# Token-major copy of the residual: 32x32 transposes on VectorE and block DMAs in place of TensorE transposes and ScalarE copies

## Chip, cores and metric

One core of a Trainium2 chip runs the whole program. The metric is the device time of one execution in microseconds (us). Engines: PE is TensorE's matmul, PEld its weight load, DVE is VectorE, ACT is ScalarE, POOL is GpSimd, SP is SyncE, whose queue issues most DMAs.

## What is computed

One decoder block on 512 tokens of width 1024, all in float32: a gated merge of a convolution branch and differential attention, added to the residual, then a SwiGLU feed-forward part, added again, and a last RMSNorm. The change touches the residual between the two additions:

```
x = x + merged @ w_out[l]                                  # the residual x1

h2 = rmsnorm(x, g_ffn[l])
ff = jax.nn.silu(h2 @ w_ffn_gate[l]) * (h2 @ w_ffn_up[l])  # D_FF = 2816
x = x + ff @ w_ffn_down[l]                                 # x1 is added here
return rmsnorm(x, g_final)
```

## The kernel before

Up to the down product the kernel keeps activations feature-major: a tile has 128 features on the partitions and the 512 tokens along the free dimension, and eight such tiles hold the width of 1024. The down product comes out token-major (128 tokens on the partitions, 512 features along the free dimension), so the residual `x1`, eight feature-major tiles, is needed once more as eight token-major tiles `x1t[(n, t)]` (`n` the half of the features, `t` the block of 128 tokens). `turn_x1` (line 947) makes them while the gate and up products run; lines 1025 and 1030 read them in the down product.

**Precision.** Each float32 product is made of three matmuls on fp32r operands: every operand is split into `hi` (a rounded copy, by ACT) and `lo` (the rest, a subtraction by DVE or POOL), and hi by hi, hi by lo and lo by hi are summed in PSUM. The text calls these three matmuls a triple.

**Weights.** `w_d` is a row of 146 units of 512 KB. `emit_dma` (line 314) loads one into a `wr` buffer (3 of them) through the SP queue; `emit_split` makes `wh` by ACT and `wl` by a subtraction, on DVE from unit 64 on and so in the whole feed-forward part (4 buffers each). `next_unit` (line 342) hands out unit i, and before that issues loads up to unit i+4 and splits up to unit i+2.

**Feed-forward part.** `chunkA` (line 405) runs one pair of 128 columns, the gate's and the up's, over the 1024 features: two weight units with 24 matmuls each, into two PSUM banks, which are of tag `mm` and of tag `at` by turns (`two`, line 904). The loop over `f` of 22 such pairs (the first stands ahead of it, line 989) is at lines 992 and 993. `evac_ff` takes each result out of PSUM on DVE, applies silu on ACT, multiplies on POOL, and splits the product (ACT copy, DVE subtraction) for the down product.

**Order.** The program is written as one order per engine by a planner: `model` keeps a clock for each engine from assumed costs (0.215 us for a matmul of 512 columns), and side work is a generator (`spawn`) that yields the planner's time at which it wants to go on. `run` calls `service` before every triple, and `service` lets a generator go on whose time has come by PE's clock, or by the time for which the next triple is ready if that is later. A DMA that is issued with `nc.sync.dma_start` directly, not through `load`, does not enter the planner's clocks. Each engine, and the SP queue, carries its instructions out in the order in which they were emitted.

Of the kernel before, what the change touches and what calls it, by code (L numbers as in the profile page):

```python
# [4 lines left out]
T = 512  # L5
D = 1024
P = 128
# [161 lines left out]
def build(nw):  # L169
# [6 lines left out]
    F32, F32R = mybir.dt.float32, mybir.dt.float32r  # L176
# [3 lines left out]
    nc = bacc.Bacc("TRN2", target_bir_lowering=False, num_devices=1, dynamic_dma_scratch_size=1024)  # L180
# [11 lines left out]
    V, S, G, PE = (Engine(model, e, n) for e, n in ((nc.vector, "dve"), (nc.scalar, "act"), (nc.gpsimd, "pool"), (nc.tensor, "pe")))  # L192
    need = model.need
    clk = model.clk

    with tile.TileContext(nc) as tc, contextlib.ExitStack() as homes:  # L196
# [3 lines left out]
        with tc.tile_pool(name="cn", bufs=1) as cn, \  # L200
# [5 lines left out]
            def nm(s):  # L206
                uid[0] += 1
                return f"{s}_{uid[0]}"
# [3 lines left out]
            def tl(tag, dt=F32, w=512):  # L212
                t = home[tag].tile([P, 542 if tag == "T2" else w], dt, name=nm(tag), tag=tag, bufs=BUFS[tag])
                model.alloc(tag, BUFS[tag], t)
                live[tag] = live.get(tag, 0) + 1
                return t
# [11 lines left out]
            def psum(tag):  # L228
                t = pp.tile([P, 512], F32, name=nm(tag), tag=tag, bufs=PBUFS[tag])
                model.alloc(tag, PBUFS[tag], t)  # L230
                return t
# [12 lines left out]
            tasks, now = [], [0.0]  # L244
# [54 lines left out]
            ident = cn.tile([P, P], F32, name="ident")  # L299
# [611 lines left out]
            x1, h2 = [], []  # L911
# [33 lines left out]
            x1t = {}  # L945

            def turn_x1():
                for n in range(2):
                    for t in range(4):
                        tp = psum("cv")  # L950
                        yield now[0] + 3.0
                        for c in range(4):
                            PE.transpose(tp[:, c * P:(c + 1) * P], x1[4 * n + c][:, t * P:(t + 1) * P], ident)
                        d = tl("T4")
                        S.copy(d, tp)
                        x1t[(n, t)] = d

            gf = [tl("T4") for _ in range(2)]
            for n in range(2):
# [29 lines left out]
            run(chunkA(h2, two(0), hold, True))  # L989
            drain_tasks()  # L990
            spawn(turn_x1())
            for f in range(1, NF):
                run(chunkA(h2, two(f), evac_ff(f)))
# [85 lines left out]
```

## Time and profile before

| | |
|---|---|
| runs | median 895.67 us, 894.81 to 900.02 |
| profiled execution | 895.89 us, span 894.1 us |
| mean granted clock of TensorE | 0.996 |
| PE, DVE, ACT, POOL busy, share of the span | 98%, 64%, 41%, 33% |
| gate and up products from `f` = 1 on (start of the transposes' stage) | 533.1 us to about 765 us |
| DMA, mean over the span | 95 GB/s |

The span runs from the first instruction of the program to the last; the rest of the execution lies around it. An engine's busy share is a mean over stages with different limits, so the stage of the change is read by itself, in windows of some 30 us. The chain is the work that ended last, followed back from the end; an instruction that isn't in it has time to spare. In the rows, PE's matmuls overlap: what one costs is read from the distance between starts or from the chain, not from its own duration. All lines of the program's compute appear as L142, since one helper records them; the tiles' names tell them apart (`T` stands for every activation tile, `at`, `mm`, `cv` for PSUM).

### The profile page before, as it was taken

What the parts mean: (1) busy time and instruction counts of PE and PEld (TensorE: products, weight loads), DVE (VectorE), ACT (ScalarE), POOL (GpSimd) and SP (SyncE); (2) the same over time, 40 slices, a digit from 0 to 9 for tenths busy, and PEclk for the clock granted to TensorE, in tenths of its full rate; (3) what the DMA queues carried; (4) which work ended last, traced back from release to release, by engine and by line L of the source; (5) the groups of instructions that cost most, each with busy time, mean ns of one, the idle gap of its engine ahead of it and who ended that gap; (6) DMA issues with size and microseconds to landing.
All of it is one profiled execution on the core that took longest, in us unless ns stands there. A gap on an engine that the chain in (4) does not pass through costs nothing.

```text
span 894.1 us, 11318 instructions
## 1 busy us (share of the span) xinstructions
PE 877.9 (98%) x4246; PEld 732.0 (82%) x4246; DVE 570.4 (64%) x961; ACT 368.9 (41%) x619; POOL 296.5 (33%) x370
## 2 busy tenths in 40 slices
PE   9999999999999999999999999999999999999996
PEld 7778989888888887688888888888888888888885
DVE  6699889889999899966765643433344444323323
ACT  7332236666666775433633433322233332221312
POOL 3785576667766357564000010111111111000001
PEclk9999999999999999999999999999999999999998
DMA  8223222222212222132224432222222222422302
GB/s 281 90 103 118 91 75 72 73 71 71 71 48 95 71 71 95 48 118 74 88 98 141 142 118 94 95 95 95 95 95 95 95 95 94 141 95 71 118 24 95
DMA packets 26584, 85.21 MB, mean 95 GB/s; under 512 B 3088, under 2 KB 4368, under 8 KB 26528
## 3 DMA queue, kind: packets, MB, share of 16 engines
q1 hardware_dynamic: 25376, 82.52, 27.0%
q10 hardware_dynamic: 1152, 1.97, 0.6%
q8 instruction: 33, 0.54, 0.2%
q14 instruction: 23, 0.19, 0.1%
HBM read 82.38 MB, written 2.10 MB: 94 GB/s over the span
## 4 chain that ended last, share of the span: by engine, by line
PE 86%; DVE 8%; ACT 3%; issue 1%; DMA 1%; SPq 0%; POOL 0%; POOLq 0%; ACTq 0%; DVEq 0%
PE mm L142 54%; PE at L142 28%; DVE T L142 5%; PE cv L142 4%; ACT T L142 2%; DVE cv L142 2%; DVE kz L142 1%; DMA wr<-wall 1%; DMA T<-xT 1%; ACT wh L142 0%; SPq L234 0%; POOL T L142 0%; ACT L142 0%; DVE sm L142 0%; POOLq L196 0%
## 5 line engine op out<-in xcount | busy, mean ns | idle before, releaser
L142 PE MATMUL mm<-T,wh 128*128 128x512 f32 x1360 | 425.9, 394 | 1.3 <-DVE T L142 1.3
L142 PEld LDWEIGHTS mm<-T,wh 128*128 128x128 f32 x1360 | 251.5, 189 | 55.7 <-issue 3.4
L142 PE MATMUL mm<-T,wl 128*128 128x512 f32 x680 | 266.1, 391 | 0.0
L142 POOL TENSOR_TENSOR wl<-wr,wh 128x256 fp32r<-128x256 f32 x244 | 189.5, 812 | 127.4 <-ACT wh L142 121.1
L142 ACT CAST wh<-wr 128x1024 fp32r<-128x1024 f32 (+1 forms) x151 | 149.7, 1016 | 82.1 <-PE mm L142 36.5
L142 POOL TENSOR_TENSOR T<-T,T 128x256 f32<-128x256 f32 (+1 forms) x97 | 91.4, 952 | 239.1 <-DVE T L142 221.9
L142 DVE SCALAR_TENSOR_TENSOR cv<-T,vec_sb,cv 128x512 f32<-128x512 f32 x232 | 160.6, 747 | 0.1
L142 PE MATMUL at<-T,wh 128*128 128x512 f32 x496 | 153.3, 390 | 0.0
L142 PEld LDWEIGHTS mm<-T,wl 128*128 128x128 f32 x680 | 128.0, 188 | 28.1 <-DVE wl L142 0.2
L142 DVE TENSOR_TENSOR wl<-wr,wh 128x1024 fp32r<-128x1024 f32 (+1 forms) x91 | 102.5, 1152 | 70.8 <-ACT wh L142 70.4
L142 DVE TENSOR_TENSOR T<-T,T 128x512 fp32r<-128x512 f32 (+2 forms) x115 | 88.9, 774 | 57.8 <-ACT T L142 56.2
L142 ACT CAST T<-T 128x512 fp32r<-128x512 f32 (+2 forms) x112 | 67.5, 618 | 122.0 <-POOL T L142 77.4
L142 PEld LDWEIGHTS at<-T,wh 128*128 128x128 f32 x496 | 92.7, 188 | 18.9
L142 DVE TENSOR_TENSOR T<-mm,T 128x512 f32<-128x512 f32 (+2 forms) x77 | 52.4, 683 | 81.1 <-PE mm L142 74.1
L142 PE MATMUL mm<-wh,T 128*128 128x256 f32 (+1 forms) x432 | 100.9, 316 | 0.0
L142 ACT ACTIVATE T<-T 128x512 f32<-128x512 f32 (+1 forms) x73 | 44.3, 622 | 130.9 <-DVE T L142 130.8
L142 PE MATMUL at<-T,wl 128*128 128x512 f32 x248 | 96.8, 390 | 0.0
L142 ACT ACTIVATE T<-T,sm 128x128 f32<-128x128 f32 (+3 forms) x100 | 55.9, 561 | 69.0 <-DVE sm L142 64.0
L142 PEld LDWEIGHTS mm<-wh,T 128*128 128x128 f32 x432 | 73.2, 190 | 5.5
L142 DVE TENSOR_TENSOR T<-at,T 128x512 f32<-128x512 f32 (+4 forms) x59 | 38.2, 650 | 59.7 <-PE at L142 54.9
L142 PE MATMUL mm<-wl,T 128*128 128x256 f32 (+1 forms) x216 | 68.2, 316 | 0.0
L142 PEld LDWEIGHTS at<-T,wl 128*128 128x128 f32 x248 | 46.6, 188 | 9.8
(90 smaller groups left out, 639.7 us busy)
## 6 DMA issues: line engine op xcount, KB each, us to landing
wr<-wall SPq DMA_DIRECT2D x144, 512.0 KB, 3.2
T<-xT SPq DMA_DIRECT2D x16, 256.0 KB, 4.4
wr<-wall SPq DMA_DIRECT2D x8, 128.0 KB, 4.4
out<-T SPq DMA_DIRECT2D x4, 256.0 KB, 2.0
out<-T ACTq DMA_DIRECT2D x4, 256.0 KB, 2.8
T<-cs ACTq DMA_DIRECT2D x2, 256.0 KB, 4.6
T<-gfin SPq DMA_DIRECT2D x2, 256.0 KB, 4.6
T<-mask ACTq DMA_DIRECT2D x1, 256.0 KB, 6.1
```

The lines of the kernel that those rows point to most:

```text
L142: r = f(*args, **kw)
```

## The change

`turn_x1` no longer uses PE, PSUM and ACT. All eight token-major tiles are allocated at once. For each feature-major tile `x1[i]`, DVE transposes each 32x32 block by itself (`V.transpose`, 128x512, into one of four buffers `y`): the block at block-row `a` and block-column `b` then holds 32 tokens on its partitions, but stands where it stood, at partitions 32a. 64 DMAs for each tile, 512 in all, carry the blocks (32 partitions by 128 bytes, 4 KB) to their places in `x1t`. They are issued on the SP queue, four at a time, with a yield of 1.1 us of the planner's clock after each four; ahead of each tile the generator yields to at least 1.0 us later and to the planner's DVE clock.

```diff
@@ -947,13 +947,19 @@
             def turn_x1():
                 for n in range(2):
                     for t in range(4):
-                        tp = psum("cv")
-                        yield now[0] + 3.0
-                        for c in range(4):
-                            PE.transpose(tp[:, c * P:(c + 1) * P], x1[4 * n + c][:, t * P:(t + 1) * P], ident)
-                        d = tl("T4")
-                        S.copy(d, tp)
-                        x1t[(n, t)] = d
+                        x1t[(n, t)] = tl("T4")
+                for i in range(8):
+                    yield max(now[0] + 1.0, clk["dve"])
+                    y = sb.tile([P, T], F32, name=nm("y"), tag="y", bufs=4)
+                    V.transpose(y, x1[i])
+                    for a in range(4):
+                        c = i % 4 * P + 32 * a
+                        for b in range(16):
+                            r, t = b % 4, b // 4
+                            nc.sync.dma_start(x1t[(i // 4, t)][32 * r:32 * r + 32, c:c + 32],
+                                              y[32 * a:32 * a + 32, 32 * b:32 * b + 32])
+                            if r == 3:
+                                yield now[0] + 1.1
```

## Rows read from the trace of the kernel before

**Rows 1.** The page: its span, and busy time of each engine.
```profile
span 894.1 us, 11318 instructions
PE 877.9 (98%) x4246; PEld 732.0 (82%) x4246; DVE 570.4 (64%) x961; ACT 368.9 (41%) x619; POOL 296.5 (33%) x370
```

**Rows 2.** Windows: busy us by engine, granted clock, DMA share, GB/s.
```profile
533.00:560.00 27.00, 27.00 (x136) 22.39 (x135) 9.87 (x12) 10.71 (x16) 3.51 (x3) 1.00 0.24 78
560.00:590.00 30.00, 30.00 (x134) 24.81 (x134) 12.71 (x14) 9.93 (x13) 2.95 (x3) 1.00 0.31 102
680.00:710.00 30.00, 30.00 (x134) 24.86 (x133) 12.62 (x14) 9.47 (x12) 3.11 (x3) 1.00 0.33 105
```

**Rows 3.** The chain: start us, us, what; from 533 us, and two later chunks.
```profile
533.09 3.40 PE at L142 x15
536.49 0.44 PE cv L142 x4
536.93 2.76 PE at L142 x12
...
569.53 10.88 PE mm L142 x48
580.41 10.88 PE at L142 x48
```

**Rows 4.** Waits of the SP queue: us, times, longest; 533 to 727, whole span.
```profile
SPq L234 <- DVE wl L142: 184.4, 35, 10.5
...
SPq L234 <- DMA wr<-wall: 3.2, 3, 2.3
SPq L234 <- DMA T<-xT: 1.3, 5, 0.5
```

**Rows 5.** Groups of instructions, 533 to 727 us: count, busy us, mean ns.
```profile
L142 PE MATMUL cv<-ident,T 128*128 128x128 f32 x32 | 4.8, 272 | 0.0
L142 ACT COPY T<-cv 128x512 f32<-128x512 f32 x8 | 4.6, 580 | 3.5 <-PE cv L142 3.3
L142 DVE TENSOR_TENSOR T<-mm,T 128x512 f32<-128x512 f32 x18 | 12.4, 692 | 36.7 <-PE mm L142 36.7
```

**Rows 6.** Groups of DVE's instructions, whole span: the stream shuffle.
```profile
L142 DVE STREAM_SHUFFLE T<-mm 128x512 f32<-128x512 f32 x16 | 11.9, 742 | 0.0
```

**Rows 7.** Timeline of one chunk: start us, us; ACT, DVE, SP.
```profile
572.28 2.00 ACT L142 CAST wh<-wr 128x1024 fp32r<-128x1024 f32 x2
573.36 2.36 DVE L142 TENSOR_TENSOR wl<-wr,wh 128x1024 fp32r<-128x1024 f32 x2 [0.26 <-ACT wh L142]
574.61 0.33 SPq L234 DMA_DIRECT2D wr<-wall  x1
575.75 0.33 SPq L234 DMA_DIRECT2D wr<-wall  x1
```

**Rows 8.** Timeline of the SP queue at the kernel's start, and at 350 us.
```profile
0.73 0.39 SPq L234 DMA_DIRECT2D gmix<-vec  x1
1.18 0.42 SPq L234 DMA_DIRECT2D T<-xT  x1
1.65 0.42 SPq L234 DMA_DIRECT2D wr<-wall  x1
2.12 0.43 SPq L234 DMA_DIRECT2D T<-xT  x1
2.59 0.43 SPq L234 DMA_DIRECT2D wr<-wall  x1
...
350.01 0.33 SPq L234 DMA_DIRECT2D wr<-wall  x1
350.43 0.35 SPq L234 DMA_DIRECT2D T<-sel  x1
350.84 0.28 SPq L234 DMA_DIRECT2D T<-sel  x1
```

**Rows 9.** DMA issues, whole span: count, KB each, median us to landing.
```profile
wr<-wall SPq DMA_DIRECT2D x144, 512.0 KB, 3.2
T<-xT SPq DMA_DIRECT2D x16, 256.0 KB, 4.4
gmix<-vec SPq DMA_DIRECT2D x1, 4.0 KB, 1.6
```

## The prediction

> **What bounds the kernel now.** I began with the page's head and its busy times [rows 1]: PE is busy for 877.9 of 894.1 us. The profiled execution took 895.89 us, 1.8 us more than its span and 0.2 us over the median of the runs, 895.67. All sums below start from 895.9.
>
> Then the windows of the stage in which the change sits, the gate and up products of the feed-forward part [rows 2]: PE is busy 30.00 of 30 us at granted clock 1.00, DVE about 12.7, ACT about 10, and the DMA engines move 0.31 of what they could. So only two things can move the time here: work taken off PE, or something that makes PE wait.
>
> The chain of work [rows 3] is PE alone. Fifteen matmuls (five triples) take 3.40 us, so a triple (hi by hi, hi by lo, lo by hi) is 0.68 us; one turn of `f` is 48 matmuls in 10.88 us, one weight unit half of that, 5.44 us. Each group of four transposes adds 0.44 us.
>
> Last came the SP queue, because the change puts 512 DMAs there. In this stage SP waits for DVE's `wl` (a free `wr` buffer) in 35 waits, 184.4 us in all [rows 4]. It is idle nearly all the time, and each load of 512 KB lands 3.2 us after its issue [rows 9]. But the queue is one line: whatever the new DMAs take on it, the next weight load behind them waits.
>
> **What is removed.** 32 transposes with their weight loads on PE [rows 5], in eight groups of 0.44 us in the chain: 8 x 0.44 = 3.5 us off the path. Eight ACT copies, 4.6 us in all [rows 5], leave an engine that is busy a third of the time; they are worth nothing, since no PE matmul waits for them.
>
> **What is added on DVE.** Eight 32x32 transposes of 128x512. The trace has none; the nearest row is the stream shuffle of the same size, 0.742 us [rows 6]: 8 x 0.742 = 5.9 us in some 186 us of a DVE that is 42% busy. Below: the other 128x512 operations of this stage, 0.69 us [rows 5]. Above, I allow double, 12 us, which DVE's idle time still covers. Counted as nothing. If DVE were late, PE would feel it through PSUM, and there each chunk takes the other tag, so a late evacuation has about a chunk to hide in.
>
> **What is added on SP: how many, and when.** 8 blocks x 4 x 16 = 512 DMAs of 4 KB, and SP issues them in program order among the weight loads. `turn_x1` emits four and yields for 1.1 us of the planner's clock. It is only asked between triples, which the planner counts as 0.645 us, so a group of four comes every second triple. Before each new `i` it also waits for the planner's DVE clock. That clock runs up to 5.6 us ahead after an evacuation, so I put the first group at the tenth triple of `f` = 1 and, walking through all 128 groups, get 274 triples from first to last. That is 274 x 0.68 = 186 us, with 34 weight loads among them: 15 small DMAs and one load per unit of 5.44 us.
>
> The first group's place is 533.1 + 9 x 0.68 = 539.2 us; DVE reaches its transpose after the two `wl` subtractions, which end 6.2 us into a chunk [rows 3, 7], so SP starts at about 540.3. The last group's place is 533.1 + 283 x 0.68 = 725.5. SP has 185 us.
>
> **The price of one issue.** At the start of the kernel SP issues loads back to back: 0.73, 1.18, 1.65, 2.12 us, that is 0.47 us each, of which the instruction is 0.42 to 0.43 [rows 8]. The bytes don't matter: the row of `gmix`, 4 KB as in a small DMA here, costs 0.39 and the load after it starts 0.45 later. These have 128 partitions; the new ones have 32. Two loads of 8 partitions cost 0.35 and, behind another of its kind, 0.28 [rows 8]; with the gap that is 0.33 us. A load of 128 partitions that finds the queue idle costs 0.33, or 0.38 with the gap [rows 8]. So the bounds are 0.33 and 0.47. I take 0.47: `gmix` is the row with the same bytes, every back-to-back load of the start shows that price and a single row the low one. What makes the second 8-partition load cheap, its own size or that of the DMA ahead of it, the rows don't tell.
>
> [...]
>
> **The sum.** SP needs 512 x 0.474 + 34 x 0.474 = 242.7 + 16.1 = 258.8 us and has 185.2, so it ends 73.6 us late. Part of it is hidden by the loads' lead. A load issued at 574.61 [rows 7] belongs to the unit that PE begins at 569.5 + 5 x 5.44 = 596.7; it lands 3.2 later [rows 9], and cast and subtraction take 2.5 more (two of each, 2.00 and 2.36 us, [rows 7]), so it is ready at 580.3 and could be 16.4 us later. The next load stands in the program at the start of the next chunk, 580.4, and its unit begins at 602.2: 16.1. I take 16.2. PE is thus late by 73.6 - 16.2 = 57.4 us, begins to starve seven or eight units in (each unit costs SP 7.6 us and so 2.1 us of the lead), and regains 3.5: +53.9 us, 949.8 for the profiled execution, 949.6 against the median. Each 0.01 us in the price of an issue is 5.1 us in the time. ACT and DVE then wait for late loads too, but the same loads hold PE first. The copies themselves are read only after 800 us, by the down product: nothing to pay there.
>
> **Rivals.**
> *The cheap issue.* If a 32-partition DMA behind another costs like the 8-partition one, 0.335 us, SP needs 171.5 + 13 = 185 us, is never late, and only PE's saving is left: 892.4, not slower. It decides below about 0.37 us per issue, where 546 issues fill the 185.2 us and the lead of 16.2. For it: the row of 0.28. Against it: that row stands alone, and 32 partitions are four times its eight. [...]
>
> *The middle.* If the price is that of an issue into an idle queue, 0.378 us: 193.5 + 13.6 (34 loads at 0.40) = 207, late by 22, less the lead of 16.2: 5.7 - 3.5 = +2, 898 us. With a wait of some 0.2 us behind each load of 512 KB (next rival) another 7: up to 906. For it: the backlog that makes 0.33 into 0.42 may shrink with the partitions.
>
> *Landing, not issue.* SP waits for the landing of an earlier transfer in five cases of `T<-xT` and three of `wr` [rows 4]: the program uses eight completion semaphores in turn for its transfers, so no more than eight are open. At 0.474 us that allows 3.8 us per landing. `gmix` landed in 1.6, loads behind others in 4.4 [rows 9]. If small DMAs behind the weight loads took 4.4 on average, an issue would come every 0.55 us: 281.6 + 18.7 - 185.2 - 16.2 - 3.5 = +95, 991 us. Against it: only one DMA in sixteen is a big one.
>
> *Order between writers.* If the blocks of one `x1t` tile had to wait for one another, 512 x 1.6 + 16 = 835 us, less the same 205 (185.2, 16.2 and 3.5): near 1526. Against it: at the start four loads fill column slices of one `wr` tile and SP issues them every 0.95 us, long before the first landed [rows 8].
>
> **How the numbers follow.** The full price, 0.45; the middle, 0.33; the cheap issue, 0.10; landing, 0.10; order, 0.02. The likeliest gives 950, and its own range is 943 to 958 (0.01 us either way in the price, 4 us in the lead). The range must reach to the cheap issue, since the three cases without landing and order hold 0.88: 892 to 960. About 1%, 9 us, can be told from no change. Slower by more: the full price, landing, order, and a third of the middle, 0.68. Within 1%: the rest of the middle and the cheap issue, 0.31. Faster by more than 1% needs 9 us where the chain offers 3.5: 0.01.
>
> **What would show it.** In the stretch 540 to 800 us, the SP queue should hold DMA issues without idle time, 0.47 us apart, the weight loads among them 7.6 us apart and not 5.44, and the chain should pass from PE to DMA `wr` and the SP queue from about 580 us on. PE's busy share there falls to about 0.7; it should be back at 1.0 before the down product. The rest of the chain should be as before. The granted clock should stay at 1.00, as in all rows of the stage [rows 2]. [...]

## The result

The changed kernel takes 1038.23 us (median of six, 1036.21 to 1039.98) against 896.55 of before, ratio 1.157 (1.155 to 1.159): 142 us slower. The prediction was 950, with 892 to 960 as its range. The direction and the place were right, the size was not.

**Profile after.** First the page's lines on the span, the busy engines, the chain and the DMA issues (out, engine, count, KB each, median us to landing). They answer to [rows 1] and [rows 9].

```profile
span 1038.2 us, 11777 instructions
PE 936.4 (90%) x4214; PEld 756.9 (73%) x4214; DVE 572.7 (55%) x969; ACT 367.9 (35%) x611; POOL 296.4 (29%) x370
...
PE mm L142 36%; SPq L959 28%; PE at L142 14%; DVE T L142 5%; PE cv L142 3%; SPq L234 2%; ACT T L142 2%; DVE cv L142 1%; DMA wr<-wall 1%; DVE kz L142 1%; ACT wh L142 1%; DMA T<-xT 0%; DVE wl L142 0%; POOL T L142 0%; ACT L142 0%
...
wr<-wall SPq DMA_DIRECT2D x144, 512.0 KB, 3.3
T<-y SPq DMA_DIRECT2D x512, 4.0 KB, 1.7
```

Line 959 is the new `dma_start`. 28% of the chain, some 290 us, are its issues on the SP queue; before, the chain was PE's in this stage [rows 3]. The transfers themselves are not the matter: a small one lands 1.7 us after its issue, and a load of 512 KB still in 3.3.

The windows of the stage (busy us and count by engine, granted clock, DMA share, GB/s) answer to [rows 2]:

```profile
543.00:575.00 32.00, 32.00 (x143) 26.50 (x142) 11.48 (x15) 7.66 (x10) 3.88 (x3) 1.00 0.17 49
...
600.00:700.00 100.00, 74.57 (x238) 55.02 (x237) 21.67 (x26) 15.64 (x19) 6.38 (x5) 0.80 0.20 57
700.00:800.00 100.00, 71.90 (x243) 52.37 (x242) 24.48 (x29) 17.74 (x21) 6.38 (x5) 0.86 0.21 61
800.00:880.00 80.00, 57.39 (x190) 41.48 (x190) 17.02 (x21) 12.54 (x16) 5.11 (x4) 0.83 0.20 59
```

PE works without a pause until 575 us and is busy for about 73% of the time after 600; part of that share is a lower granted clock (0.80 to 0.86), under which the matmuls were longer (`at<-T,wh` 0.502 us in the mean in 600 to 700, against 0.390 in 533 to 727 us of before). The SP queue's timeline shows what it waits for (start, us, instructions, count):

```profile
639.53 6.29 SPq L959 DMA_DIRECT2D T<-y  x10
645.92 0.53 SPq L234 DMA_DIRECT2D wr<-wall  x1
646.49 10.00 SPq L959 DMA_DIRECT2D T<-y  x16
656.59 0.53 SPq L234 DMA_DIRECT2D wr<-wall  x1
```

No idle time; sixteen small issues take 10.00 us, and from one weight load to the next are 10.67 us, where PE needs one every 5.44. Ten issues in 6.29 us and sixteen in 10.00 are 0.63 us apiece, not the 0.47 of [rows 8]. The tile `y` (duration ns min/median/max, first and last start) says the same of all 512, and gives DVE's transpose:

```profile
L959 SPq DMA_DIRECT2D T<-y x512: 507/589/2133, 543.1 to 892.9; - x171
L142 DVE STREAM_TRANSPOSE y<-T x8: 700/704/706, 542.3 to 831.5; 128x512 f32<-128x512 f32 x8
```

And the waits of the other engines in 580 to 880 us (engine, for whom, us in total, times, longest) show the way from the queue to PE: the cast waits for its load, the subtraction for the cast, the matmul for both. SP's own waits in that window are one of 0.2 us.

```profile
DVE wl L142 <- ACT wh L142: 198.7, 29, 10.6
ACT wh L142 <- DMA wr<-wall: 197.2, 30, 10.8
...
PEld at L142 <- ACT wh L142: 43.7, 13, 5.7
PE at L142 <- ACT wh L142: 38.2, 13, 5.3
```

Two questions were left: is the issue price the whole of the loss, and why is it 0.633 us.

### The profile page after: what moved, and what is told of

The parts are those of the page before. It is cut to its first block, busy times and chain, and to the rows that moved or that the text cites. A ratio compares the mean times of both kernels' runs of the same rounds, so it can differ in the third digit from the quotient of the medians.

```text
span 1038.2 us, 11777 instructions
## 1 busy us (share of the span) xinstructions
PE 936.4 (90%) x4214; PEld 756.9 (73%) x4214; DVE 572.7 (55%) x969; ACT 367.9 (35%) x611; POOL 296.4 (29%) x370
## 4 chain that ended last, share of the span: by engine, by line
PE 53%; SPq 30%; DVE 7%; issue 4%; ACT 3%; DMA 2%; POOL 0%; POOLq 0%; ACTq 0%; DVEq 0%
PE mm L142 36%; SPq L959 28%; PE at L142 14%; DVE T L142 5%; PE cv L142 3%; SPq L234 2%; ACT T L142 2%; DVE cv L142 1%; DMA wr<-wall 1%; DVE kz L142 1%; ACT wh L142 1%; DMA T<-xT 0%; DVE wl L142 0%; POOL T L142 0%; ACT L142 0%
## 5 line engine op out<-in xcount | busy, mean ns | idle before, releaser
L142 PE MATMUL mm<-T,wh 128*128 128x512 f32 x1360 | 443.1, 408 | 38.3 <-ACT wh L142 36.8
L142 PEld LDWEIGHTS mm<-T,wh 128*128 128x128 f32 x1360 | 261.4, 197 | 100.9 <-ACT wh L142 43.0
L142 PE MATMUL mm<-T,wl 128*128 128x512 f32 x680 | 276.0, 406 | 3.5 <-DVE wl L142 3.3
L142 PE MATMUL at<-T,wh 128*128 128x512 f32 x496 | 170.1, 427 | 38.2 <-ACT wh L142 38.2
L142 PEld LDWEIGHTS mm<-T,wl 128*128 128x128 f32 x680 | 132.8, 195 | 40.4 <-DVE wl L142 11.4
L142 PEld LDWEIGHTS at<-T,wh 128*128 128x128 f32 x496 | 102.7, 210 | 65.8 <-ACT wh L142 44.1
L142 PE MATMUL at<-T,wl 128*128 128x512 f32 x248 | 108.2, 436 | 7.5 <-DVE wl L142 7.3
L142 PEld LDWEIGHTS at<-T,wl 128*128 128x128 f32 x248 | 52.0, 210 | 26.2 <-DVE wl L142 15.1
L142 PE MATMUL at<-T,T 128*128 128x256 f32 (+4 forms) x224 | 46.9, 305 | 2.3 <-DVE T L142 1.0
```

The costliest lines, as they stand in the source:

```text
L142: r = f(*args, **kw)
```

## Experiments

My theory after the result: the SP queue's length sets the time, as forecast, and only the price was wrong. The rivals: something beside the issues costs (DVE's transposes, the small packets, their landing, PE's lower clock); and for the price, four properties in which these DMAs differ from the loads I had taken it from: both ends in SBUF, fewer partitions, a change of partitions, short runs.

### The price by itself

A program of DMAs alone, in groups of one shape, back to back, 24 to a group (gf 8, gg 16). The cut shows the DMA of each group; the loops around them, the tiles and the store group `out` are left out:

```diff
+                nc.sync.dma_start(ga[:, c(i)], x_d[0:P, c(i)])
+                nc.sync.dma_start(gb[0:32, c(i)], x_d[0:32, c(i)])
+                nc.sync.dma_start(gc[:, c(i)], src[:, c(i)])
+                nc.sync.dma_start(gd[0:32, c(i)], src[0:32, c(i)])
+                nc.sync.dma_start(ge[32:64, c(i)], src[0:32, c(i)])
+                nc.sync.dma_start(gf[32:64, c(i, 256)], src[0:32, c(i, 256)])
+                nc.sync.dma_start(g4[32:64, :, i, :], s4[0:32, :, i, :])
...
+                nc.scalar.dma_start(gk[32:64, c(i)], src[0:32, c(i)])
```

`x_d` is in DRAM, the others in SBUF; `c(i)` is the i-th slice of 128 bytes, `c(i, 256)` of 1 KB, and `g4` and `s4` take four slices each (gg). ge is the DMA of the change.

> A program of DMAs alone, so its output is zeros and a few copied blocks: groups of back-to-back issues on the SP queue, one shape to a group. The changed kernel's issues of 32 partitions x 128 bytes, SBUF to SBUF, come 0.633 us apart, against 0.474 for loads of 128 partitions from DRAM. Theory 'both ends in SBUF': the price goes with the source; 32 partitions from DRAM (gb) cost 0.47 or less, and SBUF to SBUF (gc, gd, ge) 0.63 whatever the partitions. Rival 'few partitions': gb costs 0.63 too, gc 0.47. Rival 'other partitions': gd (partitions 0 to 31 onto themselves) costs 0.47, ge (onto 32 to 63) 0.63. Rival 'short runs': gf (1 KB runs) 0.47, all groups of 128-byte runs 0.63, ga and gb too. gg (four runs of 128 bytes per partition in one DMA): 0.63 if the price is one per instruction, about 2.5 if it goes with the runs. gk is ge from the ACT queue.

The groups' rows (duration ns min/median/max, first and last start us); from the end of one issue to the start of the next are another 45 ns or so (ge: 24 starts from 60.3 to 74.9, 0.635 apart, of which 0.588 the instruction):

```profile
L37 SPq DMA_DIRECT2D ga<-x x24: 328/587/617, 1.6 to 16.9; - x24
L40 SPq DMA_DIRECT2D gb<-x x24: 311/419/605, 17.6 to 28.9; - x24
L43 SPq DMA_DIRECT2D gc<-src x24: 570/599/601, 29.4 to 44.2; - x24
L46 SPq DMA_DIRECT2D gd<-src x24: 516/588/603, 44.8 to 59.7; - x24
L49 SPq DMA_DIRECT2D ge<-src x24: 588/588/590, 60.3 to 74.9; - x24
L52 SPq DMA_DIRECT2D gf<-src x8: 588/589/590, 75.5 to 80.0; - x8
L57 SPq DMA_DIRECT2D gg<-src x16: 598/599/667, 80.6 to 90.3; - x16
L59 SPq DMA_DIRECT2D out<-src x24: 419/420/587, 91.0 to 101.8; - x24
L62 SPq DMA_DIRECT2D gi<-src x24: 624/624/760, 102.3 to 117.8; - x24
L65 SPq DMA_DIRECT2D gj<-x x24: 269/293/560, 118.5 to 127.0; - x24
```

32 partitions from DRAM cost 0.419, from SBUF 0.588. Neither a change of partitions (gd, ge) nor longer runs (gf) nor four runs in one DMA (gg) matter, and 8 partitions, cheap from DRAM (gj, 0.293, as in [rows 8]), are the dearest from SBUF (gi, 0.624). Three rivals fall; "both ends in SBUF" stands, but for ga, a load that cost 0.587. While it ran, the ACT queue was issuing gk, from 4.0 to 19.3 us: ga's issues up to 7.3 us took at most 0.44, those behind them about 0.59, and gb's from 20.1 us on took 0.42. So a second program, with ga's shape alone (ha), other partition counts, and one group from the GpSimd queue:

> A second program of DMAs alone, its output zeros and copied blocks. In the first, ga (128 partitions x 128 bytes from DRAM) came 0.633 us apart while the ACT queue issued gk beside it. ha is ga without that: theory 'two queues share something', 0.47; rival 'a strided load of 128 rows costs more', 0.63. hb and hc are SBUF to SBUF with 64 and 16 partitions: 0.63 to 0.65 if the price goes with both ends in SBUF. he and hd are loads of 16 and 64 partitions: 0.46 to 0.47; the group to DRAM with 128 partitions, 0.47. hf, alone at the end, is the changed kernel's DMA issued from the GpSimd queue, whose price no run has shown.

```profile
L37 SPq DMA_DIRECT2D ha<-x x24: 328/430/432, 1.6 to 12.7; - x24
L40 SPq DMA_DIRECT2D hb<-src x24: 554/595/596, 13.2 to 27.9; - x24
L43 SPq DMA_DIRECT2D hc<-src x24: 579/587/592, 28.5 to 43.0; - x24
L51 SPq DMA_DIRECT2D hd<-x x24: 533/595/598, 66.6 to 81.3; - x24
L54 POOL DMA_DIRECT2D hf<-hd x24: 496/498/628, 83.5 to 95.5; - x24
```

Alone, the load costs 0.430, so the ACT queue's issues beside it made it dearer. SBUF to SBUF stays at 0.59 with 64 and 16 partitions. But hd, a load of 64 partitions, which I had expected at 0.42, cost 0.595. A third program looked at that:

> A third program of DMAs alone (output zeros and copied blocks), because loads of 64 partitions from DRAM (hd) cost 0.639 us where 16, 32 and 128 cost 0.46 to 0.47, which 'both ends in SBUF' does not explain. ja repeats hd at the start: 0.64 if it is the shape, 0.47 if it was the place in that program. jb writes partitions 64 to 127, jc has runs of 1 KB, jd 96 partitions, jg 48, jf 32 onto partitions 32 to 63; the group to DRAM has 64. Theory '64 partitions are special': ja, jb, jc 0.64, the others 0.46 to 0.48. Rival 'the price stays at the level that the work ahead of it set': whichever groups follow one another alike.

```profile
L37 SPq DMA_DIRECT2D ja<-x x24: 568/595/600, 1.6 to 16.3; - x24
L57 SPq DMA_DIRECT2D jg<-x x24: 420/421/421, 87.0 to 97.7; - x24
L51 SPq DMA_DIRECT2D out<-src x24: 516/595/596, 60.5 to 75.1; - x24
```

It is the shape: 64 partitions cost 0.595 at the start too, onto partitions 64 to 127, with runs of 1 KB, and in a store to DRAM; 48 cost 0.421, 96 0.424. The medians of all groups, in us:

| partitions | 8 | 16 | 32 | 48 | 64 | 96 | 128 |
|---|---|---|---|---|---|---|---|
| DRAM to SBUF | 0.293 | 0.418 | 0.419 | 0.421 | 0.595 | 0.424 | 0.430 |
| SBUF to DRAM | | | 0.420 | | 0.595 | | 0.430 |
| SBUF to SBUF | 0.624 | 0.587 | 0.588 | | 0.595 | | 0.599 |

With both ends in SBUF an issue cost 0.587 to 0.624 in every shape measured. Why that is, and why 64 partitions cost the same with one end in DRAM, stays open.

The medians hide one thing: the first issue of a cheap group still costs about what the dear group ahead of it did. 16 partitions behind 16 from SBUF to SBUF:

```profile
43.66 0.58 SPq L46 DMA_DIRECT2D he<-x  x1
```

From the second on, he is at 0.42; the first of the store group in the first program (0.587) and the first of 96 and of 32 partitions in the third (0.581, 0.582) do the same. So the issue times here went with the DMA ahead too. The prediction had left open whether its cheap 8-partition row came from its own size or from the DMA ahead: gj's 24 of 8 partitions, behind gi's 0.624, have 0.293 as their median and 0.560 as their longest.

### The sum with another price

The same 512 DMAs at the same places in the program, but from DRAM: they carry blocks of the final gain, so the token-major copy is not made. The price changes, to about the one that the prediction used, and the DMAs no longer wait for DVE's transposes:

```diff
-                                              y[32 * a:32 * a + 32, 32 * b:32 * b + 32])
+                                              gf_d[32 * a:32 * a + 32, 32 * b:32 * b + 32])
```

> The changed kernel with another source for the 512 DMAs: blocks of 32 partitions x 128 bytes from the gain in DRAM in place of y, so the token-major copy is wrong. Same number, places in the program, queue and destination; only the price of an issue differs, 0.464 us as measured for such loads. Theory (the sum of the prediction was right and its price wrong): SP needs 512 x 0.464 + 34 x 0.47 = 254 us from 540, so the last load inside is issued near 791, 68 late, less a lead of 16 and PE's 3.5: +48, 940 to 950. Rival (something beside the issue price costs, such as the small packets, the landing or PE's lower clock): over 970.

949.47 us, ratio 1.058 (1.055 to 1.061), with packets of the same size and number, the same destinations and a granted clock of 0.93 to 0.97 in the stage.

```profile
L959 SPq DMA_DIRECT2D T<-gfin x512: 310/419/1821, 539.3 to 801.3; - x171
```

With a price near its own the prediction's sum comes out, so the sum was sound and its price was wrong. That it comes out to within a us is in part luck: the small issues came 0.464 apart and not 0.474, 5 us less; seven long ones of 1.1 to 1.8 us gave back about 7; the queue worked for 262 us, where 259 were put.

### Half of the DMAs

```diff
-                for i in range(8):
+                for i in range(4):
...
+                for n in range(1, 2):
+                    for t in range(4):
+                        tp = psum("cv")
...
```

The features of `n` = 0 go by DVE and DMAs, those of `n` = 1 by PE and ACT as before.

> Half of the change: features 0 to 511 (n = 0) by DVE and 256 DMAs, n = 1 by PE and ACT as before. Theory (SP's lateness at the last load among the DMAs, less the lead): 256 x 0.633 + 17 x 0.57 = 172 us from 543, place in the program 631, so 84 late, less 16 and 1.8 for half of PE's saving: +66, 962. Rival (loss in proportion to the DMAs, 141.7 / 2): +71, 967. Rival (a loss by the lower clock that needs long starving): under 950.

964.45 us, ratio 1.075 (1.072 to 1.078), 2.5 over the account's 962. The account's 962 lies too near to a mere half of the loss (967) to part the two, but the rival of a loss by the lower clock that needs long starving (under 950) falls.

### No DMAs

```diff
-                    y = sb.tile([P, T], F32, name=nm("y"), tag="y", bufs=4)
+                    y = tl("T4")
                     V.transpose(y, x1[i])
+                    x1t[(i // 4, i % 4)] = y
...
```

> The changed kernel without its 512 DMAs: DVE's transposes go straight into the x1t tiles, so the blocks stay where they are and the down product adds wrongly placed values. Theory (the DMA issues are the whole loss): 892 us, before less the 3.5 us of PE's transposes, ratio 0.996. Rival (DVE's transposes or the lost PSUM and ACT steps cost something by themselves): over 897.

892.19 us, ratio 0.994 (0.993 to 0.996); the spans differ by 3.4 us (890.7 against 894.1), as the chain's eight groups of 0.44 [rows 3] say. The medians of the runs differ by 5.5, between runs of before that lie 4.6 us apart among themselves. The kernel leaves out every block move (sixteen yields stand in place of the loops over `a` and `b`), so the blocks stay where DVE put them. So DVE's transposes are free, PE's saving is about the forecast one, and the DMAs are the whole loss.

### Two queues

```diff
-                            nc.sync.dma_start(x1t[(i // 4, t)][32 * r:32 * r + 32, c:c + 32],
+                            (nc.sync, nc.scalar)[b % 2].dma_start(x1t[(i // 4, t)][32 * r:32 * r + 32, c:c + 32],
```

> The changed kernel with every second DMA issued from the ACT queue. Theory 'the length of the SP queue sets the time': SP has 256 x 0.633 + 20 = 182 us for 186, so the weight loads stay on time; but ACT's own instructions stand behind 162 us of issues on its queue, and casts wait: ACT needs about 162 + 65 = 227 us for 186 us of PE, less the lead of 16: +21 us, 910 to 920. If ACT's sequencer issues while the engine computes, less: 892 to 900. Rival 'the DMA engines or their landing set the pace': as the changed kernel, 1038.

923.09 us, ratio 1.029 (1.027 to 1.031). Most of the loss goes when half of the issues leave the queue of the weights, so neither the DMA engines nor landing set the pace of the changed kernel. The rest was expected to be ACT's, and the time is 3 us over that expectation. SP's row of `y`, ACT's waits in 540 to 770 us, and the whole chain by line:

```profile
L959 SPq DMA_DIRECT2D T<-y x256: 507/589/1138, 540.5 to 767.3; - x128
...
ACT wh L142 <- DMA T<-y: 82.6, 16, 7.3
ACT T L142 <- DMA T<-y: 62.7, 23, 5.0
...
PE mm L142 41%; PE at L142 15%; DMA wr<-wall 6%; DVE T L142 6%; SPq L959 5%; DMA T<-y 5%; ACTq L959 5%; PE cv L142 4%; ACT T L142 2%; ACT wh L142 2%; DVE cv L142 1%; DVE kz L142 1%; SPq L234 1%; DVE y L142 1%; DMA T<-xT 1%
```

145 us in which ACT's engine stood idle behind its queue's small DMAs, casts among what came late. In this kernel the landing of small DMAs is in the chain, with as large a share as the issues of either queue, so landing does count here. How much of the rest is issue and how much the semaphores that both queues use in turn (the DMA records of before and after name the same eight for both) was not separated. An issue on SP costs 0.589 as in the changed kernel, though ACT issues beside it: the slowing that ga met is not seen between DMAs with both ends in SBUF.

### Four runs in one DMA

Four tiles of a half are transposed into one wide `y`, and one DMA carries a block of each, since gg's four runs cost no more than one:

```diff
-                    y = sb.tile([P, T], F32, name=nm("y"), tag="y", bufs=4)
+                    y = sb.tile([P, 4 * T], F32, name=nm("y"), tag="y", bufs=1)
...
+                            yield now[0] + 1.1
+                            nc.sync.dma_start(
+                                x1t[(n, t)].rearrange("p (i q) -> p i q", i=4)[32 * r:32 * r + 32, :, 32 * a:32 * a + 32],
+                                y.rearrange("p (i q) -> p i q", i=4)[32 * a:32 * a + 32, :, 32 * b:32 * b + 32])
```

> The same copy with 128 DMAs in place of 512: four tiles of a half are transposed into one wide y, and one DMA carries the blocks of all four (32 partitions, four runs of 128 bytes). One DMA every second triple, 3.8 per weight unit. Theory 'price per instruction', 0.63: 81 us of issues and 20 of loads in 186 us, all under the loads' lead: 892 us, ratio 0.996, the best of the versions. Rival 'price by rows or runs', about 2.5 us per DMA: as the changed kernel, 1030 to 1040. Between: at 1.2 us per DMA 154 + 20 us still fit in 186, so any price up to some 1.3 us gives 892.

893.04 us, ratio 0.9954 (0.9941 to 0.9967): half a per cent faster than before, and 145 us faster than the changed kernel. 128 issues, by its row of `y`; and one of its windows:

```profile
L960 SPq DMA_DIRECT2D T<-y x128: 585/599/1664, 544.4 to 726.6; - x128
```

```profile
560.00:590.00 30.00, 30.00 (x134) 24.86 (x133) 12.45 (x14) 7.71 (x10) 3.04 (x3) 1.00 0.39 119
```

The price per instruction is that of the changed kernel, a quarter of the number fits beside the loads, and PE does not wait, at granted clock 1.00.

## Why the prediction was wrong in size and right in kind

**The step that failed is the price of one issue.** It put 0.33 to 0.47 us as bounds and took 0.474. Measured were 0.588 and the gap of 0.045, 0.633. The rows behind the bounds [rows 8] were loads from DRAM, all of them; the trace of before holds no DMA with both ends in SBUF. Partitions and bytes were discussed, the two ends were not, though that was the property in which no row was like the new DMA. 0.47 was the dearest row shown and not an upper bound: nothing in the rows excluded a dearer issue (the trace of before holds two weight loads of 0.87 and 0.70 us, at 619 and 706 us), and the range should have reached up for it as it reached down for the cheap one.

**The rest of the sum holds to a few us, term by term.** In the chain of the changed kernel the last late load is the one before the last eight small DMAs (the chain's longest pieces there: start us, us, what):

```profile
887.94 3.38 DMA wr<-wall
891.42 1.05 ACT wh L142
892.50 1.24 DVE wl L142
893.78 5.30 PE mm L142 x22
```

Its place in the program is triple 280, by the prediction's walk at 533.1 + 280 x 0.68 = 723.5 us. It is 164.4 late; less the lead of 16.2, less 3.5 for PE: 144.7. The spans differ by 1038.2 - 894.1 = 144.1. The SP queue worked from 543.1 to 893.5, 350 us against the predicted 259: 512 x 0.159 = 81 for the price, 3 for the loads (0.57 against 0.474), and 7 for seven issues that took 1.0 to 2.1 us (the row of `y` has 2133 ns as its longest). Each of the seven starts within 0.5 us of a 16 KB transfer of instructions in the trace's DMA records (at 567.1, 611.8, 664.2, 723.8, 772.6, 820.8 and 883.1 us); that the one holds up the other was not tested. SP also began 3 us later than put, with DVE's transpose from 542.3 the last thing that it waited for. And the prediction took SP's lateness at its last issue, which would be 893.5 - 725.5 = 168.0; the last eight small DMAs stand behind that load, so this counts 3.6 us too many. Together 81 + 3 + 7 + 3 - 4 = 90 us, and the measured 144.1 is 90 over the predicted 53.9. The number and places of the groups, the 34 loads, the lead and PE's saving need no correction.

**What hides what.** DVE's transpose took 0.704 us where 0.742 was put [rows 6], eight of them 5.6 us, and the kernel without DMAs shows that they cost nothing. ACT's eight copies gave nothing, as said.

**The rivals.** The cheap issue and the middle fall with the price. Landing falls: 1.7 us and at most 4.6, under the eight issues of 0.63 (5.1 us) that a semaphore has until it comes round. The DMA records of before and after name eight semaphores in turn, and at the start of the kernel before, the load at 6.07 us follows the landing of the eighth ahead of it, issued at 2.12 and landed 3.9 later. Order between writers falls: 512 issues run 0.633 apart. One of these DMAs takes little to issue beside its landing, 0.59 against 1.7 us; 512 of them in a queue that weights share took 350 us with the loads.

**What would show it.** The queue without idle time, the chain from PE to SP's queue and the loads: as written. PE at 0.7 (0.73) and the first wait at about 580 us (581) agree by luck. Loads 10.67 us apart leave PE work for 5.44 / 10.67 = 0.51 of the time, and its 238 matmuls in 600 to 700 us are, at the 10.88 us for 48 of [rows 3], 54 of 100 us; they were busy for 74.57 us, at a granted clock of 0.80. At the prediction's own price the lead would have lasted until about 600 us: seven or eight units of 7.6 us on SP's queue from 540.3. So it does in the kernel that reads from DRAM, where PE first waits at 599.93 us:

```profile
599.93 0.50 PE L142 MATMUL at<-T,wl 128*128 128x512 f32 x1 [0.33 <-DVE wl L142]
```

Not as written: loads 10.67 and not 7.6 us apart, and the granted clock, which fell to 0.80 to 0.86. The changed kernel's PE timeline shows it after a wait of 3.94 us (start, us, matmuls):

```profile
580.99 0.50 PE L142 MATMUL at<-T,wl 128*128 128x512 f32 x1 [0.53 <-DVE wl L142]
...
590.24 0.73 PE L142 MATMUL at<-T,wh 128*128 128x512 f32 x2 [3.94 <-ACT wh L142]
591.50 0.80 PE L142 MATMUL at<-T,wl 128*128 128x512 f32 x1 [0.53 <-DVE wl L142]
592.09 1.05 PE L142 MATMUL at<-T,wh 128*128 128x512 f32 x2
592.95 0.63 PE L142 MATMUL at<-T,wl 128*128 128x512 f32 x1
593.37 1.05 PE L142 MATMUL at<-T,wh 128*128 128x512 f32 x2
594.23 0.63 PE L142 MATMUL at<-T,wl 128*128 128x512 f32 x1
594.65 0.70 PE L142 MATMUL at<-T,wh 128*128 128x512 f32 x2
595.19 0.40 PE L142 MATMUL at<-T,wl 128*128 128x512 f32 x1
595.43 0.62 PE L142 MATMUL at<-T,wh 128*128 128x512 f32 x2
```

Triples start 1.28 us apart for a while, not 0.68, at a granted clock of 0.50 from 591.50 to 594.20 us; from 594.70 to 597.00 it is 0.98. By these rows that lengthens the unit by some 2 us (three triples, 0.6 each), and by the account it costs nothing, since SP's next load comes 10.67 us after the last. The sum closes to 0.6 us without a term for it; no run changed the clock alone, so this is by the account and not shown by itself.

## What to carry to other kernels

Count the instructions of a change on every queue, SP's too, and multiply by a price from a row with the same kind of ends and about the same number of partitions; where no row has them, the dearest row is not an upper bound, and the range must stay open upwards. A queue that also carries prefetches has only the prefetch's lead as slack (here 16 us); past that, each microsecond of issue was one of the kernel here (144.7 by the account, 144.1 measured). Issues from SBUF to SBUF were paid by the instruction, not by the byte or the run (one run of 128 bytes 0.588 us, one of 1 KB 0.589, four of 128 bytes 0.599): pack blocks that share their partitions into one DMA before moving them off PE.

## What the runs showed of the hardware that was not expected

- On the SP queue, by the medians of groups of one shape, an issue of a DMA with both ends in SBUF took 0.587 to 0.624 us (8, 16, 32, 64 and 128 partitions), with one end in DRAM 0.418 to 0.430 (16, 32, 48, 96 and 128); four runs per partition in one DMA took 0.599, one 0.588.
- 64 partitions were an exception: 0.595 us also from and to DRAM, where loads of 48 and 96 took 0.421 and 0.424.
- A second queue made an issue dearer: loads of 128 partitions on SP went from 0.430 to 0.587 while ACT issued SBUF to SBUF at 0.602 (one pair of groups). SBUF to SBUF on SP stayed at 0.589 beside ACT's.
- The first issue of a cheap shape behind a dear one took about the dear price in four groups: 0.578 to 0.587 where the median of its group was 0.418 to 0.424.
- From the GpSimd queue the change's DMA took 0.498 us of POOL (one group of 24).
